# Attention scores in four groups of 32 queries with four heads as rows, in a Griffin-style block on one core

## The chip, the cores and the metric

The kernel runs on one core of a Trainium2 chip. The metric is the device time of one execution in microseconds (us); of the kernel before there are three timed runs, and one further execution that was profiled.

## The reference, cut to what matters

One layer of a decoder over 2048 tokens of width 1024: an RMS norm, one wide projection, two branches (a gated causal convolution and sliding-window attention), each with its own output projection, a gated merge, an output projection and the residual. The change touches the attention alone:

```python
q = rms_norm(q.reshape(b, s, 16, 64), q_norm_g)          # 16 query heads of 64
k = rms_norm(k.reshape(b, s, 4, 64), k_norm_g)           # 4 key/value heads: 4 query heads share one
# per block of 128 queries: keys of this block and of the block before it
scores = einsum('bnqhgd,bnkhd->bnhgqk', qb, kb) * scale
valid = (diff >= 0) & (diff < 128) & (k_pos >= 0)         # diff = q_pos - k_pos
scores = where(valid, scores, -1e30)
m = maximum(max(scores, axis=-1), sink)                   # sink: one learned number per query head
p = exp(scores - m)
p = p / (sum(p) + exp(sink - m))
out = einsum('bnhgqk,bnkhd->bnqhgd', p, vb)
```

A query sees its own position and the 127 before it, so 128 keys in all.

## The kernel before, in words

All matmuls are in fp32r with both operands split in a high and a low part; a product is the sum of three matmuls (high by high, high by low, low by high). The tokens are worked in two halves `t` of 1024. In each half a list of units (`SEQ0`, `SEQ1`) sets which slice of the wide weights is multiplied next; a unit is seven products of 12 matmuls (L475), written by a two-level block scheme that saves one product in eight. `run` counts a tick per product, and `put(n, f)` hangs every other step on a tick. What is recorded stands in each engine's queue in just this order: the schedule is manual, the queues are in order.

The attention is 32 pairs per half (`j`: key/value head, 0 to 3; `b`: block of 128 queries, 0 to 7), 64 blocks in all. `AT0` and `AT1` give the tick `n` of each block, and the steps of a block are at fixed distances from it: `att_load` at n-5, `att_scores` at n, `att_exp` at n+1, `att_norm` at n+2, `att_flip` at n+2, `att_back` at n+4, `att_turn` at n+9, `att_low` at n+10, `att_values` at n+13, `att_out` at n+14, `att_sum` at n+15.

The queries come out of their units with head dimension on rows; `parts` (in `fin_q`) splits them and writes them to DRAM (`q2d`, DMAs on the GpSimd queue, high part on rows 0 to 63, low part on 64 to 127). `k_out` does so for the keys (`kd`), both parts twice so that they fill 128 rows. `att_load` (SP queue) fetches a block's queries and keys. Before, `q2d` keeps groups of 64 queries, and a row of scores is one of two heads by 64 queries; the other pair of heads (`c`) goes to other columns. `att_scores` then runs, for each half `h` of the block's queries, one matmul for the low parts of the keys, with both pairs of heads on the 128 rows and keys that stand block-diagonally in the tiles `lows` (zeros elsewhere), 2 x 192 columns wide, and two matmuls of 192 columns with the high parts of the keys against both parts of the queries. 192 columns are 64 queries' window: 64 keys more than a query sees. `copy_predicated` puts the scores of the first 64 columns in place of the masked ones of the last 64, so that `exp` and all behind it work on 128 columns per row.

`att_exp` computes the sink's term and the weights (four `exp` with `accum_out`), `att_norm` divides, `att_flip` turns 32x32 blocks on VectorE and writes them to DRAM, `att_back` reads them turned, `att_low` masks with four `affine_select` on GpSimd, `att_values` multiplies with the values, `att_out` copies the result out of PSUM.

The rms of the queries: `rms` collects sums of squares, and `by_query` lays the factors out in the tile `rq`, one per score row. For the first three `j` of the first half (`BY_PE`) the queries are turned by TensorE, and `by_query` has to move factors between partitions; for the others `squares_sum` adds two halves of the head dimension.

Of the kernel before, what the change touches and what calls it, by code (L numbers as in the profile page):

```python
# [10 lines left out]
I32 = mybir.dt.int32  # L11
# [42 lines left out]
TURN_WAIT = 3  # L54

# [46 lines left out]
def block_kernel(  # L102
# [49 lines left out]
    q2d = [[dram.tile([P, 2 * NB, 2, 2, HD], F32, name=f"q2d{t}_{j}") for j in range(NKV)]  # L152
# [32 lines left out]
    mask_f = slot([P, 2, HD], F32, "mask_f")  # L185
    for h in range(2):
        nc.gpsimd.affine_select(
            out=mask_f[:, h, :], in_=ones[:, 0:HD], pattern=[[1, HD]], compare_op=ALU.is_gt,
            fill=0.0, base=h * HD, channel_multiplier=-1)
    mask_i = consts.tile([P, HD], I32, name="mask_i")  # L190
    for h in range(2):
        nc.gpsimd.tensor_copy(mask_i[HALVES[h]], mask_f[HALVES[h], h, :])
    negc = consts.tile([P, HD], F32, name="negc")
# [3 lines left out]
    sink_r = cols[:, C_S:NC].rearrange("p (j h c) -> p j h c", h=2, c=2)  # L197
    nsink_r = consts.tile([P, NKV, 2, 2], F32, name="nsink_r")
# [591 lines left out]
    def squares_sum(a, name):  # L790


        got = small.tile([P, 32], F32, tag="sm", name=f"{name}_g")
        both = small.tile([P, 32], F32, tag="sm", name=f"{name}_b")
        av = a.rearrange("p (m s) -> p s m", s=2)
        for k in range(4):
            nc.scalar.copy(got[QUADS[k]], av[QUADS[k ^ 1], k % 2])
        return both, [
            lambda k=k: nc.vector.tensor_tensor(
                out=both[QUADS[k]], in0=av[QUADS[k], k % 2], in1=got[QUADS[k]], op=ALU.add)  # L800
            for k in range(4)]

    def fin_q(t, j):
# [38 lines left out]
        def parts(i, q, qt):  # L842
# [5 lines left out]
            for e in range(2):  # L848
                for half, src in ((LH, hi), (UH, lo)):
                    nc.gpsimd.dma_start(  # L850
                        q2d[t][j][half, q * 2 * HB : (q + 1) * 2 * HB, i, e, :],
                        src[HALVES[e]].bitcast(F32).rearrange("p (b x) -> p b x", x=HD))
# [9 lines left out]
        def by_query(r):  # L862

            rq = consts.tile([P, 2, HB, 2, 2], F32, tag="rq", bufs=4, name=f"rq{t}_{j}")
            if not by_pe:
                vec.tensor_copy(rq, r.rearrange("p (c q b h) -> p q b h c", c=2, q=2, h=2))
# [3 lines left out]
            for e in range(2):  # L870
                for h in range(2):
                    vec.tensor_copy(rq[HALVES[e], :, :, h, :], rv[HALVES[h], :, :, :, e])
# [71 lines left out]
    lows = [consts.tile([P, 2, 2 * P], F32R, name=f"lows{i}") for i in range(2)]  # L944
    for kz in lows:
        nc.gpsimd.memset(kz.bitcast(F32), 0.0)

    def att_load(t, j, b):
        nm = f"{t}_{j}_{b}"
        gb = t * NB + b  # L950
        kz = lows[(j * NB + b) % 2]
        q2 = slot([P, 2, 2, P], F32R, f"q2_{nm}")
        nc.sync.dma_start(
            q2.bitcast(F32).rearrange("p h c x -> p (h c x)"),
            q2d[t][j][:, 2 * b : 2 * b + 2].rearrange("p h c e x -> p (h c e x)"))
# [15 lines left out]
        return q2, kq, kz  # L971
# [18 lines left out]
    def att_scores(t, j, b, ld):  # L990
        first = t * NB + b == 0
        nm = f"{t}_{j}_{b}"
        q2, kq, kz = ld
        rv = rqs[t, j][:, b // HB, b % HB]
        sp = ps_s.tile([P, 2, 2, 2 * P], F32, tag="s", name=f"s{nm}")
        for h in range(2):
            skip = (2 - h) * HD if first else 0
            keys = slice(h * HD + skip, (h + 3) * HD)
            nc.tensor.matmul(
                sp[:, h, :, skip : 3 * HD], lhsT=kq[:, 1, h * P : (h + 1) * P], rhs=kz[:, :, keys],  # L1000
                start=True, stop=False)
            for c in range(2):
                nc.tensor.matmul(  # L1003
                    sp[:, h, c, skip : 3 * HD], lhsT=q2[:, h, c, :], rhs=kq[:, 0, keys],
                    start=False, stop=c == 1)
        sg = sp.rearrange("p h c k -> p (h c) k")
        m = mask_i.unsqueeze(1).to_broadcast([P, G, HD])
        if first:
            vec.copy_predicated(
                sg[:, :, 2 * HD : 3 * HD], m, negc.unsqueeze(1).to_broadcast([P, G, HD]))  # L1010
            vec.tensor_copy(sg[:, 0:2, HD : 2 * HD], negc.unsqueeze(1).to_broadcast([P, 2, HD]))
# [3 lines left out]
        vec.tensor_reduce(out=st[:, 0], in_=sg[:, :, HD : 3 * HD], axis=AX.X, op=ALU.max)  # L1015
# [717 lines left out]
```

## Time and profile before

| | |
|---|---|
| three timed runs | 1894.27, 1896.89, 1897.73 us; median 1896.89 |
| the profiled execution's own time | 1898.81 us |
| its span, first to last instruction | 1897.1 us |
| busy: TensorE, its weight loads | 99%, 83% |
| busy: VectorE, ScalarE, GpSimd | 81%, 52%, 38% |
| DMA | 434.74 MB, mean 229 GB/s |

In rows of the profile PE is TensorE's matmul, PEld its weight load, DVE VectorE, ACT ScalarE, POOL GpSimd, SPq the SP queue. A row's form `128*128 128x192` says that the matmul uses 128 x 128 of the array and writes 128 rows of 192 columns. Line numbers are those of the kernel before.

### The profile page before, as it was taken

How to read it: one execution, taken by the hardware profiler on the slowest of the kernel's cores; microseconds unless marked ns; L12 is line 12 of the kernel's file. 1: busy time of each engine (PE TensorE's matmuls, PEld its weight loads, DVE VectorE, ACT ScalarE, POOL GpSimd, SP SyncE). 2: the span in 40 equal slices, each digit the busy share in tenths (PEclk: the TensorE clock that was granted, in tenths of full speed). 3: DMA queues.
4: the chain of work that ended last, by engine and by line, in shares of the span. 5: the costliest groups of instructions: out<-in, count | busy, mean ns of one | idle time of the engine just before them, and what ended most of it. 6: DMA issues, size and time to landing. Idle time of an engine off the chain costs nothing.

```text
span 1897.1 us, 27925 instructions
## 1 busy us (share of the span) xinstructions
PE 1884.8 (99%) x8670; PEld 1567.5 (83%) x8670; DVE 1537.5 (81%) x2527; ACT 989.6 (52%) x1993; POOL 720.7 (38%) x1022
## 2 busy tenths in 40 slices
PE   9999999999999999999999999999999999999999
PEld 7888888888888887778887888888888888888887
DVE  7989888789777789887579988888888779886654
ACT  7665554567675354345445645556566446444321
POOL 1472454556765121121055445655666311121000
PEclk9999999999999999999999999999999999999999
DMA  8585466689988878989367657767989869889653
GB/s 305 123 211 178 141 175 190 183 258 283 261 239 231 298 267 293 317 290 301 114 186 183 182 174 198 209 182 214 246 234 266 269 237 344 323 273 279 223 174 110
DMA packets 260548, 434.74 MB, mean 229 GB/s; under 512 B 33264, under 2 KB 124400, under 8 KB 260400
## 3 DMA queue, kind: packets, MB, share of 16 engines
q1 hardware_dynamic: 202848, 314.13, 50.8%
q0 software_dynamic: 57408, 118.80, 24.7%
q8 instruction: 69, 1.13, 0.3%
q14 instruction: 79, 0.65, 0.1%
q10 hardware_dynamic: 144, 0.03, 0.0%
HBM read 278.43 MB, written 154.40 MB: 228 GB/s over the span
## 4 chain that ended last, share of the span: by engine, by line
PE 81%; DVE 5%; issue 5%; DMA 5%; POOL 2%; ACT 1%; SPq 0%; DVEq 0%; POOLq 0%; ACTq 0%
PE Y L475 29%; PE Vcv L475 5%; PE Xcv L475 4%; PE Xb L475 2%; PE Xga L475 2%; PE Vb L475 2%; PE Xz L475 2%; PE Vga L475 2%; PE Vz L475 2%; PE Vo L475 2%; PE Xo L475 2%; PE po L1093 2%; PE Vyb L475 2%; PE Xgb L475 2%; PE Xyb L475 2%
## 5 line engine op out<-in xcount | busy, mean ns | idle before, releaser
L1055 POOL DMA_DIRECT2D x<-fd x256 | 142.8, 595 | 79.8 <-DMA fd<-f 30.8
L1076 POOL TENSOR_SCALAR_AFFINE_SELECT xh<-xh 64x512 fp32r<-64x512 f32 x64 | 67.2, 1051 | 137.4 <-DVE xl L257 103.4
L1028 ACT ACTIVATE p<-s,st,rq 128x128 f32<-128x128 f32 x256 | 112.9, 451 | 5.1 <-DMA fd<-f 3.3
L1048 POOL DMA_DIRECT2D fd<-f x64 | 38.6, 604 | 170.6 <-DVE f L257 161.3
L475 PE MATMUL Xcv<-oph,wcv_ah 128*128 128x512 f32 x256 | 79.5, 392 | 0.0
L1109 POOL DMA_DIRECT2D od<-o x64 | 68.9, 1084 | 20.1 <-DMA od<-o 18.1
L1299 POOL DMA_DIRECT2D md<-thyb x32 | 27.4, 873 | 100.6 <-DVE thyb L257 69.8
L1076 POOL TENSOR_SCALAR_AFFINE_SELECT xl<-xl 64x512 fp32r<-64x512 f32 x64 | 63.3, 989 | 4.4
L1076 POOL TENSOR_SCALAR_AFFINE_SELECT yp<-xl 64x512 fp32r<-64x512 f32 x64 | 58.0, 906 | 3.1
L1076 POOL TENSOR_SCALAR_AFFINE_SELECT yp<-yp 64x512 fp32r<-64x512 f32 x64 | 54.7, 855 | 4.2
L475 PEld LDWEIGHTS Xcv<-oph,wcv_ah 128*128 128x128 f32 x256 | 47.3, 188 | 9.4
L257 DVE SCALAR_TENSOR_TENSOR y<-u,cols,y 128x512 f32<-128x512 f32 x64 | 51.8, 810 | 3.7 <-ACT y L1138 2.5
L850 POOL DMA_DIRECT2D q2d<-q_h x64 | 44.2, 691 | 27.9 <-ACT q_h L845 22.8
L257 DVE TENSOR_TENSOR opa<-ina,opa 128x512 fp32r<-128x512 f32 x56 | 36.1, 686 | 20.5 <-ACT opa L292 20.5
L257 DVE TENSOR_TENSOR p<-p,st 128x512 f32<-128x512 f32 x64 | 50.1, 784 | 2.6
L357 ACT CAST wcv_sh<-wcv_raw 128x1024 fp32r<-128x1024 f32 x16 | 16.9, 1054 | 67.1 <-DVE wcv_raw L257 67.1
L1028 ACT ACTIVATION_READ_ACCUMULATOR p<-s,st,rq 128x1 f32 x256 | 51.1, 200 | 0.0
L850 POOL DMA_DIRECT2D q2d<-q_l x64 | 44.1, 689 | 16.8 <-DVE q_l L257 10.2
L475 PE MATMUL Xcv<-oph,wcv_al 128*128 128x512 f32 x128 | 49.8, 389 | 0.0
L1003 PEld LDWEIGHTS s<-kq,q 128*128 128x128 f32 x256 | 45.9, 189 | 2.2
L257 DVE STREAM_TRANSPOSE f<-p 128x512 f32<-128x512 f32 x64 | 45.4, 710 | 2.7 <-DVE p L257 0.2
L257 DVE TENSOR_TENSOR opc<-inc,opc 128x512 fp32r<-128x512 f32 x56 | 36.2, 686 | 13.7 <-ACT opc L292 13.6
(768 smaller groups left out, 6606.1 us busy)
## 6 DMA issues: line engine op xcount, KB each, us to landing
wcv_raw<-in_w_in SPq DMA_DIRECT2D x32, 512.0 KB, 4.2
q<-q2d SPq DMA_DIRECT2D x64, 256.0 KB, 4.7
v<-vd SPq DMA_DIRECT2D x128, 128.0 KB, 4.5
fd<-f POOLq DMA_DIRECT2D x64, 256.0 KB, 3.9
x<-fd POOLq DMA_DIRECT2D x256, 64.0 KB, 3.4
gd<-th SPq DMA_DIRECT2D x64, 256.0 KB, 3.5
wq_raw<-in_w_in SPq DMA_DIRECT2D x16, 512.0 KB, 5.2
q2d<-q_h POOLq DMA_DIRECT2D x64, 128.0 KB, 4.6
```

The costliest lines, as they stand in the source:

```text
L257: r = f(*args, **kw)
L357: return (lambda: nc.scalar.copy(hi, src), lambda: vec.tensor_tensor(out=lo, in0=src, in1=hi.bitcast(F32), op=ALU.subtract))
L475: nc.tensor.matmul(ps, lhsT=w[:, j, :], rhs=b[:, m, :], start=start and j == 0 and i == 0, stop=j == KP - 1 and i == 2, skip_group_check=n ...
L850: nc.gpsimd.dma_start(q2d[t][j][half, q * 2 * HB : (q + 1) * 2 * HB, i, e, :], src[HALVES[e]].bitcast(F32).rearrange("p (b x) -> p b x", x ...
L1003: nc.tensor.matmul(sp[:, h, c, skip : 3 * HD], lhsT=q2[:, h, c, :], rhs=kq[:, 0, keys], start=False, stop=c == 1)
L1028: nc.scalar.activation(out=p[:, i, :], in_=sg[:, i, HD : 3 * HD], func=AF.Exp, bias=st[:, 1, i : i + 1], scale=rv[:, i // 2, i % 2 : i % 2 ...
L1048: nc.gpsimd.dma_start(fd, f)
L1055: nc.gpsimd.dma_start(x[QUADS[k]], src[k])
L1076: nc.gpsimd.affine_select(out=d4, in_=s4, pattern=[[0, 2], [-32 * sg, 2], [0, G], [-sg, 32]], compare_op=ALU.is_gt if prev else ALU.is_ge, ...
L1093: nc.tensor.matmul(po[:, cs], lhsT=v2[:, kind, :], rhs=xx[:, :, h * HD : (h + 1) * HD], start=h == 0 and n == 0, stop=n == 2, skip_group_c ...
L1109: put(tick[0] + ADD_WAIT, lambda: nc.gpsimd.dma_start(to, o[UH].rearrange("p c e q -> p (c e) q"), accum_op=ALU.add))
L1299: nc.gpsimd.dma_start(md[t][k, :, hs(q)], m, accum_op=ALU.add)
```

## The change

Scores are computed for four groups `s` of 32 queries. A row is now one of the four heads by 32 queries, a group's window is 160 keys, and there are two matmuls a group: 128 rows (high and low parts of the queries by the keys' high parts, 160 columns) and 64 rows (queries' high part by the keys' low part, 160 columns). The block-diagonal tiles `lows` and the extra copy of the queries' high parts (`kq`'s second half) go; the low parts of the keys are written and read once, on 64 rows. `q2d` holds runs of 32 elements in place of 64. The masks follow: `copy_predicated` works on 4 x 32 columns. The addition that made the sink's argument goes, since `exp` takes the sink as its bias (a row has one head now). `att_flip` needs three transposes for its four heads' order, `by_query` 16 small copies on ScalarE and GpSimd in place of 4 on VectorE, `squares_sum` 8 copies on ScalarE and one addition in place of 4 and 4. The host's layout of the sinks follows.

```diff
+SLOTS = (0, 1, 2, 3)
-    q2d = [[dram.tile([P, 2 * NB, 2, 2, HD], F32, name=f"q2d{t}_{j}") for j in range(NKV)]
+    q2d = [[dram.tile([P, 4 * NB, 2, 2, 32], F32, name=f"q2d{t}_{j}") for j in range(NKV)]
...
         for e in range(2):
-            for l, src in enumerate((hi, lo)):
-                nc.gpsimd.dma_start(
-                    kd[t][2 * i + e, :, l, hs(q)].rearrange("(o d) t -> d o t", d=HD),
-                    src[HALVES[e]].bitcast(F32).unsqueeze(1).to_broadcast([HD, 2, H]))
+            nc.gpsimd.dma_start(
+                kd[t][2 * i + e, :, 0, hs(q)].rearrange("(o d) t -> d o t", d=HD),
+                hi[HALVES[e]].bitcast(F32).unsqueeze(1).to_broadcast([HD, 2, H]))
+            nc.gpsimd.dma_start(kd[t][2 * i + e, LH, 1, hs(q)], lo[HALVES[e]].bitcast(F32))
...
         for k in range(4):
-            nc.scalar.copy(got[QUADS[k]], av[QUADS[k ^ 1], k % 2])
+            i, e = divmod(k, 2)
+            for o, dst in enumerate((got, both)):
+                nc.scalar.copy(dst[QUADS[k]], a[QUADS[2 * e + o], i * 32 : (i + 1) * 32])
         return both, [
-            lambda k=k: nc.vector.tensor_tensor(
-                out=both[QUADS[k]], in0=av[QUADS[k], k % 2], in1=got[QUADS[k]], op=ALU.add)
-            for k in range(4)]
+            lambda: nc.vector.tensor_tensor(out=both, in0=both, in1=got, op=ALU.add)]
...
-                        q2d[t][j][half, q * 2 * HB : (q + 1) * 2 * HB, i, e, :],
-                        src[HALVES[e]].bitcast(F32).rearrange("p (b x) -> p b x", x=HD))
+                        q2d[t][j][half, q * 4 * HB : (q + 1) * 4 * HB, i, e, :],
+                        src[HALVES[e]].bitcast(F32).rearrange("p (b x) -> p b x", x=32))
...
-            for e in range(2):
-                for h in range(2):
-                    vec.tensor_copy(rq[HALVES[e], :, :, h, :], rv[HALVES[h], :, :, :, e])
+            for k in range(4):
+                for n, s in enumerate(SLOTS):
+                    copy = nc.gpsimd.tensor_copy if s % 2 else nc.scalar.copy
+                    copy(rq[QUADS[k], :, :, n], rv[QUADS[s], :, :, k // 2, k % 2])
...
-        for c in range(2):
-            nc.sync.dma_start(
-                kq[HALVES[c], 1].bitcast(F32).rearrange("p (h x) -> p h x", h=2),
-                q2d[t][j][LH, 2 * b : 2 * b + 2, c].rearrange("p h e x -> p h (e x)"))
...
             nc.sync.dma_start(kq[:, 0, here].bitcast(F32), kd[kt][j, :, 0, there])
-            for c in range(2):
-                nc.sync.dma_start(kz[HALVES[c], c, here].bitcast(F32), kd[kt][j, HALVES[c], 1, there])
+            nc.sync.dma_start(kq[LH, 1, here].bitcast(F32), kd[kt][j, LH, 1, there])
...
-        for h in range(2):
-            skip = (2 - h) * HD if first else 0
-            keys = slice(h * HD + skip, (h + 3) * HD)
-            nc.tensor.matmul(
-                sp[:, h, :, skip : 3 * HD], lhsT=kq[:, 1, h * P : (h + 1) * P], rhs=kz[:, :, keys],
-                start=True, stop=False)
-            for c in range(2):
-                nc.tensor.matmul(
-                    sp[:, h, c, skip : 3 * HD], lhsT=q2[:, h, c, :], rhs=kq[:, 0, keys],
-                    start=False, stop=c == 1)
+        for n, s in enumerate(SLOTS):
+            skip = P - 32 * s if first else 0
+            keys = slice(32 * s + skip, 32 * s + 5 * 32)
+            to = sg[:, n, skip : 5 * 32]
+            nc.tensor.matmul(
+                to, lhsT=q2[:, s], rhs=kq[:, 0, keys],
+                start=n % 2 == 0, stop=False, skip_group_check=n % 2 == 1)
+            nc.tensor.matmul(
+                to, lhsT=q2[LH, s], rhs=kq[LH, 1, keys],
+                start=False, stop=True, skip_group_check=n % 2 == 1)
...
-            vec.copy_predicated(sg[:, :, 2 * HD : 3 * HD], m, sg[:, :, 0:HD])
+            vec.copy_predicated(sg[:, :, 4 * 32 : 5 * 32], m, sg[:, :, 0:32])
...
-        add(st[:, 2], sink_r[:, j].rearrange("p h c -> p (h c)"), st[:, 1])
...
-        nc.scalar.activation(out=st[:, 3], in_=st[:, 2], func=AF.Exp)
+        nc.scalar.activation(out=st[:, 3], in_=st[:, 1], func=AF.Exp, bias=sink_r[:, j, 0:1])
...
-        vec.transpose(out=f, in_=p.rearrange("p g (b r) -> p b g r", r=32))
+        to = f.rearrange("p (b h s q) -> p b h s q", b=4, h=2, s=2)
+        src = p.rearrange("p (h s) (b r) -> p b h s r", s=2, r=32)
+        vec.transpose(out=to[:, 0:3, :, 0], in_=src[:, 1:4, :, 0])
+        vec.transpose(out=to[:, 3, :, 0], in_=src[:, 0, :, 0])
+        vec.transpose(out=to[:, :, :, 1], in_=src[:, :, :, 1])
...
-            d4 = dst.rearrange("p (e s) (g q) -> p e s g q", s=2, q=32)
-            s4 = src.rearrange("p (e s) (g q) -> p e s g q", s=2, q=32)
+            d4 = dst.rearrange("p g (h s q) -> p (g h) s q", s=2, q=32)
+            s4 = src.rearrange("p g (h s q) -> p (g h) s q", s=2, q=32)
             nc.gpsimd.affine_select(
-                out=d4, in_=s4, pattern=[[0, 2], [-32 * sg, 2], [0, G], [-sg, 32]],
+                out=d4, in_=s4, pattern=[[0, 2 * G], [-32 * sg, 2], [-sg, 32]],
```

How the instructions move is shown at two places. The first is TensorE's queue at the scores of block `j` = 0, `b` = 2 of the first half, between two products of a unit (`s` is the score tile, `q` and `kq` are what `att_load` brought, `Xcv` and `Y` are banks of the unit's products). Before:

```order
L475 MATMUL Xcv_2_1963<-oph_2_3_533,wcv_2_al 128x512
L999 MATMUL s_0_2_2060<-lows_151,kq_0_2_1927 128x2x192
L1003 MATMUL s_0_2_2060<-kq_0_2_1927,q_0_0_2_1925 128x192 x2
L999 MATMUL s_0_2_2060<-lows_151,kq_0_2_1927 128x2x192
L1003 MATMUL s_0_2_2060<-kq_0_2_1927,q_0_0_2_1925 128x192 x2
L475 MATMUL Y<-oph_7_0_910,wcv_2_th 128x512 x2
```

The same place after (L990 has 128 rows of operands, L993 has 64):

```order
L476 MATMUL Xcv_2_1999<-oph_2_3_533,wcv_2_al 128x512
L990 MATMUL s_0_2_2093<-kq_0_2_1964,q_0_0_2_1962 128x160
L993 MATMUL s_0_2_2093<-kq_0_2_1964,q_0_0_2_1962 128x160
L990 MATMUL s_0_2_2093<-kq_0_2_1964,q_0_0_2_1962 128x160
L993 MATMUL s_0_2_2093<-kq_0_2_1964,q_0_0_2_1962 128x160
L990 MATMUL s_0_2_2093<-kq_0_2_1964,q_0_0_2_1962 128x160
L993 MATMUL s_0_2_2093<-kq_0_2_1964,q_0_0_2_1962 128x160
L990 MATMUL s_0_2_2093<-kq_0_2_1964,q_0_0_2_1962 128x160
L993 MATMUL s_0_2_2093<-kq_0_2_1964,q_0_0_2_1962 128x160
L476 MATMUL Y<-oph_7_0_910,wcv_2_th 128x512 x2
```

Six matmuls with 1536 columns in all became eight with 1280, of two forms that alternate; the products on both sides stand where they stood.

The second is ScalarE's queue in the first half, where the factors of `j` = 0 are ready (`q_0_r` is VectorE's result, `rq` the tile by query). Before:

```order
L845 ACTIVATE q_1_1_0_h<-q_1_1_0_t,gqk 128x512
L274 ACTIVATE q_0_t<-q_0_ms 128x32
L777 ACTIVATE ptq_1_0_0_1246<-ptq_1_0_0_1246 128x512
L292 CAST k_1_1_h<-pbk_1_1_1252 128x512
L577 COPY q_2_0_1_t<-Vq_2_1138 128x512
```

The same place after:

```order
L845 ACTIVATE q_1_1_0_h<-q_1_1_0_t,gqk 128x512
L275 ACTIVATE q_0_t<-q_0_ms 128x32
L873 COPY rq_0_1241<-q_0_r 32x8 x8
L778 ACTIVATE ptq_1_0_0_1258<-ptq_1_0_0_1258 128x512
L293 CAST k_1_1_h<-pbk_1_1_1264 128x512
L578 COPY q_2_0_1_t<-Vq_2_1138 128x512
```

Eight copies that wait for VectorE's result now stand ahead of the evacuations of PSUM (`ptq`, `pbk`, `Vq`); eight more stand in GpSimd's queue, and VectorE's four are gone.

More of the change, by code (lines that the diff above doesn't have):

```diff
@@ L183, in block_kernel @@
     nc.gpsimd.memset(ones, 1.0)
-    mask_f = slot([P, 2, HD], F32, "mask_f")
-    for h in range(2):
+    mask_f = slot([P, 4, 32], F32, "mask_f")
+    for k in range(4):
         nc.gpsimd.affine_select(
-            out=mask_f[:, h, :], in_=ones[:, 0:HD], pattern=[[1, HD]], compare_op=ALU.is_gt,
-            fill=0.0, base=h * HD, channel_multiplier=-1)
-    mask_i = consts.tile([P, HD], I32, name="mask_i")
-    for h in range(2):
-        nc.gpsimd.tensor_copy(mask_i[HALVES[h]], mask_f[HALVES[h], h, :])
-    negc = consts.tile([P, HD], F32, name="negc")
+            out=mask_f[:, k, :], in_=ones[:, 0:32], pattern=[[1, 32]], compare_op=ALU.is_gt,
+            fill=0.0, base=k * 32, channel_multiplier=-1)
+    mask_i = consts.tile([P, 32], I32, name="mask_i")
+    for k in range(4):
+        nc.gpsimd.tensor_copy(mask_i[QUADS[k]], mask_f[QUADS[k], k, :])
+    negc = consts.tile([P, 3 * 32], F32, name="negc")
     nc.gpsimd.memset(negc, NEG)
-    sink_r = cols[:, C_S:NC].rearrange("p (j h c) -> p j h c", h=2, c=2)
-    nsink_r = consts.tile([P, NKV, 2, 2], F32, name="nsink_r")
+    sink_r = cols[:, C_S:NC].rearrange("p (j s) -> p j s", s=4)
+    nsink_r = consts.tile([P, NKV, 4], F32, name="nsink_r")
     gqk = consts.tile([P, 1], F32, name="gqk")
```

50 lines of the change are left out of this document (22 added, 28 removed).

## The prediction

> **What bounds the kernel now.** The page comes first, for who is busy; then TensorE's waits, then the long runs of its chain, then its queue around one block of scores.
>
> ```profile
> PE 1884.8 (99%) x8670; PEld 1567.5 (83%) x8670; DVE 1537.5 (81%) x2527; ACT 989.6 (52%) x1993; POOL 720.7 (38%) x1022
> PEclk9999999999999999999999999999999999999999
> PE Y L1467 <- DVE zero L176: 1.5, 1, 1.5
> ...
> PE Vya L475 <- ACT zas L1259: 0.2, 1, 0.2
> PE Y L475 <- DVE wya_tl L257: 0.2, 1, 0.2
> 883.18 5.44 PE Xga L475 x24
> 888.62 5.44 PE Vga L475 x24
> ```
>
> TensorE is busy for 99% of the span, with at least nine tenths of its clock granted in every slice. Its waits are ten rows, of which the first is the longest and these the last; none of the ten names a tile of the attention. Undisturbed, 24 matmuls of 512 columns take 5.44 us, 0.227 us each, and the chain is made of such runs. So nothing but TensorE's own instructions sets the end: what they grow by is paid in full, and a saving elsewhere brings next to nothing. What the attention costs here is the spacing of its matmuls, which their durations don't tell, since they overlap. The queue around a late block shows it, matmuls first, weight loads second:
>
> ```profile
> 1452.07 0.34 PE L999 MATMUL s<-lows,kq 128*128 128x384 f32 x1
> 1452.25 0.36 PE L1003 MATMUL s<-kq,q 128*128 128x192 f32 x2
> 1452.45 0.36 PE L999 MATMUL s<-lows,kq 128*128 128x384 f32 x1
> 1452.65 0.36 PE L1003 MATMUL s<-kq,q 128*128 128x192 f32 x2
> 1452.85 0.64 PE L475 MATMUL Xz<-oph,wz_ah 128*128 128x512 f32 x2
> 1452.07 0.37 PEld L1003 LDWEIGHTS s<-kq,q 128*128 128x128 f32 x2
> 1452.36 0.19 PEld L999 LDWEIGHTS s<-lows,kq 128*128 128x128 f32 x1
> 1452.47 0.37 PEld L1003 LDWEIGHTS s<-kq,q 128*128 128x128 f32 x2
> 1452.76 0.30 PEld L475 LDWEIGHTS Xz<-oph,wz_ah 128*128 128x128 f32 x2
> ```
>
> Each load goes out when the matmul before starts to stream. A pair of loads of 0.19 us that spans 0.37 us is 0.18 us apart: its second waits for the 384 columns to stream (384 x 0.227/512 = 0.17 us). The load after that comes 0.11 us later (1452.25 to 1452.36), the next again 0.11 (1452.36 to 1452.47). But 192 columns stream in 192 x 0.227/512 = 0.085 us: there it is no longer the columns that set the pace, it is the next matmul's weights, one load per 0.11 us. That floor decides this change.
>
> **The change part by part.** *TensorE, on the path.* Now a block takes twice 0.18 + 0.11 + 0.11 us = 0.80 us by its loads (the matmuls say 1452.85 - 1452.07 = 0.78). Afterwards there are eight matmuls of 160 columns, which stream in 160 x 0.227/512 = 0.071 us, all of them below the floor. If the floor holds for all, a block takes 8 x 0.11 = 0.88 us: 0.08 us more, though it streams 256 columns fewer. Over 64 blocks that is **+5.1 us**. No row here has a load of 64 rows, or a matmul on 64 rows: every form reads `128*128`. The 64-row load is bounded from below by nothing but the stream it hides behind (0.071 us; then a block takes 4 x 0.11 + 4 x 0.071 = 0.72 us, -4.9 us in all) and from above by what the full one takes. I take the full one, as the nearest row.
>
> The Trainium skill, "TensorE: Matmul & The Clock Gate", section "LDWEIGHTS (loading the stationary operand)", says that a weight load costs its columns divided by 1.2 GHz and not its rows, which for 128 columns is an estimated 0.107 us for 64 rows as for 128; by it the sum would be the same to within 2 us. The 0.11 us above agree for 128 rows; for 64 no run here shows it yet.
>
> *VectorE, off the path.* A block loses the sink's addition and half the elements of `copy_predicated`, and gets two more transposes of the same 512 elements.
>
> ```profile
> L257 DVE STREAM_TRANSPOSE f<-p 128x512 f32<-128x512 f32 x64 | 45.4, 710 | 2.7 <-DVE p L257 0.2
> L257 DVE COPY_PREDICATED s<-mask_i,s 128x256 f32<-128x256 int32 x60 | 25.4, 422 | 6.2 <-PE s L1003 5.7
> L257 DVE TENSOR_TENSOR st<-cols,st 128x4 f32<-128x4 f32 x64 | 17.0, 266 | 2.1
> L257 DVE SCALAR_TENSOR_TENSOR st<-st,nsink_r 128x4 f32<-128x4 f32 x64 | 13.2, 206 | 2.0
> ```
>
> Saved: 266 ns, and of 422 between 0 and 211. Added: twice an instruction's fixed part, between 0 and the 206 ns of a four-element row. Per block that is -477 to +146 ns, so -31 to +9 us over 64 blocks on an engine with 19% to spare; the strided pattern of the transposes could cost more, which no row shows. I take it as nothing on the path. If that cover were gone, the +9 us would be the price.
>
> *ScalarE, nearly off the path.* Twenty-four copies for three `rq` and four more for each of five `squares_sum`, at the 0.218 us of the row below, are 9.6 us on an engine that is half idle. What matters is that the first eight of each `rq` wait for VectorE, with evacuations queued behind:
>
> ```profile
> L797 ACT COPY q_g<-qss x20: 214/218/229, 158.3 to 1082.8; 32x32 f32<-32x32 f32 x20
> 110.83 0.23 ACT L274 ACTIVATE q_t<-q_ms 128x32 f32<-128x32 f32 x1 [1.51 <-DVE q_ms L270]
> 114.00 0.59 ACT L577 COPY q_t<-Vq 128x512 f32<-128x512 f32 x1 [1.94 <-issue]
> 111.93 0.19 DVE L288 SCALAR_TENSOR_TENSOR q_r<-q_t,q_r 128x32 f32<-128x32 f32 x1
> ```
>
> VectorE has the factors at 112.12; eight copies end at 113.9, and the square and the cast that ScalarE did meanwhile (0.6 us each) end at 115.1, so `Vq` is copied out some 1.1 us later than at 114.00. TensorE writes that bank again only after other products of 2.7 us each (12 x 0.227), which hide it. Uncovered it would be 3 x 1.1 = 3 us, once per `rq`.
>
> *GpSimd, SP and the DMAs, off the path.* The same number of `q2d` DMAs now have twice as many runs, half as long:
>
> ```profile
> L850 POOL DMA_DIRECT2D q2d<-q_h x64 | 44.2, 691 | 27.9 <-ACT q_h L845 22.8
> L1048 POOL DMA_DIRECT2D fd<-f x64 | 38.6, 604 | 170.6 <-DVE f L257 161.3
> DMA  8585466689988878989367657767989869889653
> q1 hardware_dynamic: 202848, 314.13, 50.8%
> q0 software_dynamic: 57408, 118.80, 24.7%
> q2d<-q_h POOLq DMA_DIRECT2D x64, 128.0 KB, 4.6
> kq<-q2d SPq DMA_DIRECT2D x128, 64.0 KB, 4.2
> lows<-kd SPq DMA_DIRECT2D x112, 64.0 KB, 3.5
> ```
>
> Their issue goes from 691 ns to at most 691 + (691 - 604) = 778 ns: 128 x 0.09 = 11 us of an engine that idles for 62%. SP issues 128 loads of `q2d` and half of those of `lows` less, and what they moved (8.4 + 3.7 MB of q1, whose 314 MB take 50.8% of the span, 3.07 us a MB) gives 37 us of all the queues' time back. The writes cost, at q0's average of 24.7% of 1897 us for 118.8 MB, 16.8 MB x 3.9 = 66 us; doubled runs cost between nothing and as much again. Half of these 66 us would fall in each half's query units (slices 1 to 3, at 5, 8 and 5 tenths, and about 21 to 23), where room remains. The nearest evidence that lateness there is harmless is that none of TensorE's ten waits is for a DMA. I take nothing.
>
> *The sum.* The profiled execution took 1898.81 us around a span of 1897.1; with +5.1 it is 1903.9. The median of the three timed runs lies 1.9 us lower, at 1896.89, so I forecast **1902.0 us**, 0.27% over before. What a measurement of this kernel can tell from no change is about 0.2%, 3.8 us.
>
> **The rivals.** *A, the array drains between the two forms.* In each block 128-row and 64-row matmuls alternate, eight changes of form. If a matmul of the other form must wait until the one before has left the array, each change costs up to a matmul's whole duration:
>
> ```profile
> L1003 PE MATMUL s<-kq,q x256: 221/263/277, 158.4 to 1452.7; 128*128 128x192 f32 x120, 128*128 128x64 f32 x4, 128*128 128x128 f32 x4
> L1003 PEld LDWEIGHTS s<-kq,q x256: 187/188/192, 158.4 to 1452.6; 128*128 128x128 f32 x128
> ```
>
> At 0.25 us for 160 columns (between 0.221 and 0.263) a block takes 8 x 0.25 = 2.0 us, +1.2, times 64 = +77: 1974 us. If the load can't be hidden either, 8 x (0.25 + 0.19) = 3.5 us a block, +174: 2071 us. A short drain, within the 0.04 us by which the load already outlasts the stream, would vanish in the forecast. For it: nothing here shows the two forms side by side, so nothing speaks against. Against it: the durations' ends are modelled, and back to back they cost nothing today. The Trainium skill, "TensorEngine Tiling (Array Packing)", section "Key Properties", says that changing the tiling mode, not only the tile, drains TensorE; no run here shows it, and it gives no figure. Chance 0.33, a third of it beyond 1974 us.
>
> *B, faster: the 64-row loads are cheap and the columns count.* One mechanism, in TensorE's queue: if a load of half the rows takes half the time, 0.055 us, it hides behind the 0.071 us of streaming, and the block takes the 0.72 us above: -4.9 us, 1892 us. If the short matmuls escape the floor altogether, 8 x 0.071 = 0.57 us, -0.23 x 64 = -15: 1882 us. It decides from a 64-row load under 0.09 us: then 4 x 0.11 + 4 x 0.09 = 0.80 us, as now. Against it stands that the floor of 0.11 us followed the load and not the columns in each row above. Chance 0.09.
>
> *C, the query units become the bound.* If the doubled runs double the cost of `q2d`'s writes, each half's query units have 33 us more DMA time; where 0.65 of 76 us are taken (50 us), that makes 83, and 7 us overflow into waits for weights in each half: with the +5.1, 1916 us. With late evacuations it is 1919. For it: slice 2 at 8 tenths. Against it: 37 us of other traffic go. Chance 0.08.
>
> **How the numbers follow.** The forecast has 0.50. Its own spread, from loads of 0.105 to 0.115 us a piece, is +2.6 to +7.7 us, so 1899.5 to 1904.6 us; about a quarter of it lies within 0.2%. Slower by over 0.2%: 0.37 of the forecast, all but 0.02 of A's 0.33, 0.07 of C: 0.75. Within 0.2%: 0.13 + 0.02 + 0.01, with 0.01 of B: 0.17. Faster: 0.08. The range runs from 1892, where B's milder case lies, to 1974, A without exposed loads; left out are A's worse third (0.11) and half of B (0.04).
>
> **What would show it.** In the profile after, in TensorE's queue: eight score matmuls in 0.88 us, with loads 0.11 us apart for both forms, means that the floor holds. Loads of the 64-row form closer than 0.09 us mean B. Starts of alternate forms over 0.12 us apart mean A, and the spacing is its price. TensorE waiting for a weight tile between 60 and 145 us or 975 and 1070 us means C, or for `Vq`'s bank, the copies. The forecast is wrong if a block of scores isn't within 0.05 us of 0.88 us, or if waits of TensorE beyond today's ten rows come to more than 3 us.

## The result, and the profile after

| | before | after |
|---|---|---|
| median of the runs, us | 1896.35 (4 runs) | 1989.18 (4 runs, 1986.45 to 1991.4) |
| ratio, 95% interval | 1 | 1.0487 [1.0475, 1.0499] |
| profiled execution, us (span) | 1898.81 (1897.1) | 1988.47 (1986.7) |

The changed kernel is 4.9% slower. The forecast of 1902.0 us had the sign; the time lies 15 us above the range's upper end of 1974 us.

The page of the kernel after, its line of engines and its two rows for the score matmuls (busy, mean ns of one, idle before):

```profile
PE 1971.8 (99%) x8798; PEld 1609.4 (81%) x8798; DVE 1515.7 (76%) x2572; ACT 1004.1 (51%) x2037; POOL 737.0 (37%) x1048
L993 PE MATMUL s<-kq,q 64*128 64x160 f32 (+3 forms) x256 | 85.9, 336 | 0.0
L990 PE MATMUL s<-kq,q 128*128 128x160 f32 (+3 forms) x256 | 80.1, 313 | 0.0
```

TensorE is as busy as before, at 99%, and nearly the whole difference shows up as busy time: 1971.8 - 1884.8 = 87 us. VectorE's busy time fell by 22 us, and that bought nothing. The block that the prediction showed, in TensorE's timeline of the kernel after (start, duration), matmuls first, then loads:

```profile
1539.99 0.24 PE L990 MATMUL s<-kq,q 128*128 128x160 f32 x1
1540.15 0.34 PE L993 MATMUL s<-kq,q 64*128 64x160 f32 x1
1540.42 0.34 PE L990 MATMUL s<-kq,q 128*128 128x160 f32 x1
1540.69 0.34 PE L993 MATMUL s<-kq,q 64*128 64x160 f32 x1
...
1541.77 0.34 PE L993 MATMUL s<-kq,q 64*128 64x160 f32 x1
1542.04 0.73 PE L476 MATMUL Xz<-oph,wz_ah 128*128 128x512 f32 x2
1542.61 0.39 PE L476 MATMUL Xz<-oph,wz_al 128*128 128x512 f32 x1
1540.15 0.18 PEld L993 LDWEIGHTS s<-kq,q 64*128 64x128 f32 x1
1540.42 0.19 PEld L990 LDWEIGHTS s<-kq,q 128*128 128x128 f32 x1
1540.69 0.18 PEld L993 LDWEIGHTS s<-kq,q 64*128 64x128 f32 x1
```

Two things are to be seen. The starts of alternate forms are 0.27 us apart (1540.15, 1540.42, 1540.69), not 0.11. And each load starts together with its own matmul: it did not go out while the matmul before it streamed, as the loads did in the kernel before. The block takes 1542.04 - 1539.99 = 2.05 us, where it took 0.78. The effect reaches one matmul further: the first two matmuls of `Xz`, which again have 128 rows, together take 0.73 us where they took 0.64. Added up over all 64 blocks in the two traces, from the first score matmul to the second matmul behind the block, the time went from 65.2 to 151.6 us: 86.4 of the 89.6 us by which the span grew.

The first block of each key/value head in the first half has fewer columns. There the intervals between the forms are 0.21 us at 32 columns, 0.23 at 64, 0.24 at 96 and 0.26 at 128 (the same trace): some 0.2 us that do not depend on the columns, and the streaming on top, by the 0.227 us for 512 columns.

TensorE's waits after have two rows of the attention that before's had not:

```profile
PE po L1087 <- POOL yp L1070: 1.2, 1, 1.2
PE po L1087 <- POOL xl L1070: 0.7, 1, 0.7
```

They are 1.9 us here. In the experiments they turned out to be the tip of a second cost. TensorE also waits twice for ScalarE to empty the bank `Y` (1.0 us), which it did not before.

### The profile page after: what moved, and what is told of

It is laid out like the page before. It is cut to its first block, busy times and chain, and to the rows that moved or that the text cites. A ratio compares the mean times of both kernels' runs of the same rounds, so it can differ in the third digit from the quotient of the medians.

```text
span 1986.7 us, 27990 instructions
## 1 busy us (share of the span) xinstructions
PE 1971.8 (99%) x8798; PEld 1609.4 (81%) x8798; DVE 1515.7 (76%) x2572; ACT 1004.1 (51%) x2037; POOL 737.0 (37%) x1048
## 4 chain that ended last, share of the span: by engine, by line
PE 84%; DVE 5%; DMA 4%; issue 3%; POOL 2%; ACT 1%; SPq 0%; POOLq 0%; DVEq 0%; ACTq 0%
PE Y L476 29%; PE Vcv L476 4%; PE Xcv L476 4%; PE s L993 3%; PE s L990 3%; PE po L1087 2%; PE Xgb L476 2%; PE Vgb L476 2%; PE Xb L476 2%; PE Xga L476 2%; PE Vb L476 2%; PE Xz L476 2%; PE Vga L476 2%; PE Vz L476 2%; PE Xza L476 2%
## 5 line engine op out<-in xcount | busy, mean ns | idle before, releaser
L993 PE MATMUL s<-kq,q 64*128 64x160 f32 (+3 forms) x256 | 85.9, 336 | 0.0
L990 PE MATMUL s<-kq,q 128*128 128x160 f32 (+3 forms) x256 | 80.1, 313 | 0.0
L850 POOL DMA_DIRECT2D q2d<-q_l x64 | 52.8, 824 | 46.4 <-issue 32.1
L993 PEld LDWEIGHTS s<-kq,q 64*128 64x128 f32 x256 | 46.8, 183 | 27.6 <-issue 9.3
L850 POOL DMA_DIRECT2D q2d<-q_h x64 | 52.9, 827 | 41.5 <-issue 19.1
L990 PEld LDWEIGHTS s<-kq,q 128*128 128x128 f32 x256 | 47.8, 187 | 18.0
L1070 POOL TENSOR_SCALAR_AFFINE_SELECT xl<-xl 64x512 fp32r<-64x512 f32 x64 | 57.6, 901 | 4.4
L258 DVE STREAM_TRANSPOSE f<-p 128x192 f32<-128x192 f32 (+2 forms) x192 | 53.5, 328 | 2.8 <-DVE p L258 0.2
L258 DVE SCALAR_TENSOR_TENSOR y<-u,cols,y 128x512 f32<-128x512 f32 x64 | 51.2, 801 | 3.9 <-ACT y L1132 2.7
L258 DVE COPY_PREDICATED s<-mask_i,s 128x128 f32<-128x128 int32 x60 | 17.6, 293 | 45.5 <-PE s L993 45.4
```

The source lines that it names most:

```text
L258: r = f(*args, **kw)
L850: nc.gpsimd.dma_start(q2d[t][j][half, q * 4 * HB : (q + 1) * 4 * HB, i, e, :], src[HALVES[e]].bitcast(F32).rearrange("p (b x) -> p b x", x ...
L990: nc.tensor.matmul(to, lhsT=q2[:, s], rhs=kq[:, 0, keys], start=n % 2 == 0, stop=False, skip_group_check=n % 2 == 1)
L993: nc.tensor.matmul(to, lhsT=q2[LH, s], rhs=kq[LH, 1, keys], start=False, stop=True, skip_group_check=n % 2 == 1)
L1070: nc.gpsimd.affine_select(out=d4, in_=s4, pattern=[[0, 2 * G], [-32 * sg, 2], [-sg, 32]], compare_op=ALU.is_gt if prev else ALU.is_ge, fil ...
```

## The experiments

Two explanations compete for the 87 us. **Change of form**: what costs is the step from a matmul on 128 rows to one on 64 and back, so the time follows the number of steps. **The 64-row matmul itself**: it, or its load, is slow wherever it stands, so the time follows the number of such matmuls, whatever their order. A third possibility is that neither matters, and the eight loads or the rest of the change cost it.

### One form only

The low parts' product is made on 128 rows: the keys' low parts lie in a tile whose upper half is zero.

```diff
-            nc.sync.dma_start(kq[LH, 1, here].bitcast(F32), kd[kt][j, LH, 1, there])
+            nc.sync.dma_start(kz[LH, here].bitcast(F32), kd[kt][j, LH, 1, there])
...
-                to, lhsT=q2[LH, s], rhs=kq[LH, 1, keys],
+                to, lhsT=q2[:, s], rhs=kz[:, keys],
```

> The low-part matmuls of the changed kernel run on 128 rows instead of 64 (the keys' low parts lie in a tile whose rows 64 to 127 are zero); eight matmuls of 160 columns a block, all of one form, the rest of the change as it is. Theory F (each change between the 64-row and the 128-row form costs, nothing else does): no change of form is left, so a block takes the floor of 8 x 0.11 = 0.88 us, +5 us over the kernel before: about 1902 us. Rival P (eight short matmuls that accumulate in turn on the same PSUM columns are slow in any form): stays near 1985 us. Rival R (the other parts of the change cost a share): between the two, with the part over 1902 as their price.

Measured: 1918.74 us, 1.0099 [1.0078, 1.012] of before's 1897.59. Eight matmuls of 160 columns in the same order, with eight loads, cost 70 us less than in the changed kernel. Its timeline of a late block:

```profile
1473.05 0.24 PE L995 MATMUL s<-kq,q 128*128 128x160 f32 x1
1473.13 0.28 PE L998 MATMUL s<-lows,q 128*128 128x160 f32 x1
1473.24 0.27 PE L995 MATMUL s<-kq,q 128*128 128x160 f32 x1
...
1473.80 0.28 PE L998 MATMUL s<-lows,q 128*128 128x160 f32 x1
1473.91 0.67 PE L476 MATMUL Xz<-oph,wz_ah 128*128 128x512 f32 x2
```

The floor of 0.11 us is there, and the block takes 0.86 us against the 0.88 that I had forecast. By the sum over 64 blocks that is 72.1 - 65.2 = 6.9 us. The other 14 of these 21 us, which I had not expected here either, are the second cost, below.

### Fewer changes, the same matmuls

The eight matmuls of the changed kernel in another order: four on 128 rows, then four on 64 (two changes a block); or two and two (four changes).

```diff
+        for n, l, last in [(n, 0, False) for n in range(4)] + [(n, 1, True) for n in range(4)]:
+            work[n][l](last)
```

```diff
+        for n, l, last in ((0, 0, False), (1, 0, False), (0, 1, True), (1, 1, True), (2, 0, False), (3, 0, False), (2, 1, True), (3, 1, True)):
+            work[n][l](last)
```

> The changed kernel with the same eight matmuls a block in another order: four of 128 rows, then four of 64 rows. Theory F: the changed kernel has 8 changes of form a block for +92 us, of which 5 are the floor's, so a change costs 87 / 512 = 0.17 us; here 2 changes a block remain: 5 + 64 x 2 x 0.17 = +27 us, about 1923 us. Rival S (a 64-row matmul or its weight load is slow by itself, whatever its neighbours are): the same 256 of them, unchanged near 1985 us.

> The changed kernel with its eight matmuls a block in the order two of 128 rows, two of 64, two of 128, two of 64. Theory F: 4 changes of form a block, 5 + 64 x 4 x 0.17 = +49 us, about 1945 us, halfway between the grouped order and the changed kernel on a straight line of 22 us per two changes. Rival S: near 1985 us.

| changes of form a block | kernel | us | the 64 blocks in the trace, us |
|---|---|---|---|
| 0 | one form | 1918.74 | 72.1 |
| 2 | four and four | 1933.16 | 92.0 |
| 4 | two and two | 1951.5 | 111.8 |
| 8 | the changed kernel | 1989.18 | 151.6 |

The last three have the same 64-row matmuls, so the 64-row matmul as such isn't it. The blocks (summed as above) grow by 19.9, 19.8 and 39.8 us: 9.9 us a change over 64 blocks, 0.155 us each, on a straight line. By the times it is 70.4 us from 0 to 8 changes, 0.14 us each, and the steps of 14.4, 18.3 and 37.7 us are less even, since the second cost is larger in the first two kernels: outside the blocks the four traces take 1846, 1844, 1834 and 1835 us. Both middle kernels came out above what I expected (1923 and 1945 us). The timeline of "four and four", where rows of one form are drawn together:

```profile
1490.44 0.58 PE L992 MATMUL s<-kq,q 128*128 128x160 f32 x4
1490.94 0.67 PE L995 MATMUL s<-kq,q 64*128 64x160 f32 x4
1491.55 0.73 PE L476 MATMUL Xz<-oph,wz_ah 128*128 128x512 f32 x2
1490.32 0.54 PEld L992 LDWEIGHTS s<-kq,q 128*128 128x128 f32 x4
1490.94 0.52 PEld L995 LDWEIGHTS s<-kq,q 64*128 64x128 f32 x4
```

Four loads on 64 rows of 0.18 us span 0.52: (0.52 - 0.18)/3 = 0.113 us apart, as far as the full ones, (0.54 - 0.19)/3 = 0.117. The first 64-row load stands at the start of its matmul (1490.94 both), the first full one 0.12 us ahead of its own. So it is the step from form to form that takes the load's cover away, and not the 64 rows. The Trainium skill, "TensorE: Matmul & The Clock Gate", section "LDWEIGHTS (loading the stationary operand)", has a load cost its columns and not its rows; these rows agree.

### The price, put into the kernel before

One matmul is added to each block of the kernel before, on 64 rows in the first and on 128 rows in the second, its control. It writes 64 columns that a later matmul overwrites; no part of the computation is left out.

```diff
+        nc.tensor.matmul(
+            sp[:, 0, 0, 2 * HD : 3 * HD], lhsT=kq[LH, 1, 0:P], rhs=kz[LH, 0, 2 * HD : 3 * HD],
+            start=True, stop=True)
```

```diff
+            sp[:, 0, 0, 2 * HD : 3 * HD], lhsT=kq[:, 1, 0:P], rhs=kz[:, 0, 2 * HD : 3 * HD],
```

> The kernel before with one matmul more a block, ahead of its scores: 64 rows, 64 columns, its result overwritten by the scores. Theory F (a change of form costs; from the versions with 0, 2, 4 and 8 changes a block, 70 us for 8, 0.14 us a change): 0.11 us for the matmul and 2 x 0.14 for the two changes, x 64 = +25 us, about 1922 us. Rival N (the price belongs to the new scores' accumulation or order and not to the form): +7 us, like the same matmul on 128 rows, about 1904 us.

> The control: the kernel before with the same extra matmul on 128 rows, one form throughout. One weight load at the floor, 0.11 x 64 = +7 us, about 1904 us, by both theories; near 1897 us if a short matmul hides among the others, so that the floor is no floor.

Measured: 1919.68 us on 64 rows (1.0113 [1.0098, 1.0129]) and 1903.10 on 128 (1.0029 [1.0017, 1.0041]); before took 1897.64. One more matmul costs 5.5 us, 0.085 us a block; the same one on 64 rows costs 16.6 us more. Over 2 x 64 changes that is 0.13 us a change, in a kernel that has nothing else of the change. In the timeline with the 64-row matmul:

```profile
1454.07 0.39 PE L475 MATMUL Xz<-oph,wz_al 128*128 128x512 f32 x1
1454.38 0.29 PE L996 MATMUL s<-lows,kq 64*128 64x64 f32 x1
1454.61 0.44 PE L1002 MATMUL s<-lows,kq 128*128 128x384 f32 x1
1454.89 0.36 PE L1006 MATMUL s<-kq,q 128*128 128x192 f32 x2
1454.38 0.18 PEld L996 LDWEIGHTS s<-lows,kq 64*128 64x128 f32 x1 [0.35 <-issue]
```

From the start of `Xz`'s matmul of 512 columns to that of the 64-row matmul it takes 0.31 us, not 0.23. Its weight load, for which the trace shows nothing to wait for, comes only then, after 0.35 us without a load. And it takes 0.23 us until the next 128-row matmul starts, though only 64 columns stream.

### Where the other 14 us went: GpSimd's queue

In the kernel with one form, TensorE waits longer for the masks that GpSimd makes (first fence), and the first of those masks comes later. The next fences are each kernel's rows on `q2d`'s DMAs (duration min/median/max, first and last start of both halves together; then GpSimd's idle time ahead of such DMAs, in us and times, that no event explains) and on the masks:

```profile
PE po L1092 <- POOL yp L1075: 3.1, 2, 1.9
PE po L1092 <- POOL xl L1075: 2.1, 2, 1.3
PE po L1092 <- POOL xh L1075: 1.7, 2, 1.1
```

The kernel before:

```profile
L850 POOL DMA_DIRECT2D q2d<-q_h x64: 687/687/729, 63.1 to 1069.2; - x64
  issue: 2.9, 6
L1076 POOL TENSOR_SCALAR_AFFINE_SELECT xh<-xh x64: 742/762/1690, 188.9 to 1483.3; 64x512 fp32r<-64x512 f32 x64
```

The kernel with one form:

```profile
L850 POOL DMA_DIRECT2D q2d<-q_h x64: 822/824/862, 63.3 to 1086.7; - x64
  issue: 48.2, 50
L1075 POOL TENSOR_SCALAR_AFFINE_SELECT xh<-xh x64: 739/762/1673, 197.8 to 1504.4; 64x512 fp32r<-64x512 f32 x64
```

An issue takes 0.82 us where it took 0.69; the doubled runs are all that the change did to these DMAs. The 48.2 us of waits don't follow from that. The last `q2d` DMA of the first half starts at 176.7 us instead of 149.5 (from the traces), GpSimd's part of the copies into `rq` stands behind it, and the masks behind those, the first of them 8.9 us late.

The waits for masks, 6.9 us, are only part of the 14. Behind them the clock that TensorE was granted fell to half, for 3.4 and for 6.8 us. A slice of the page is 48 us long, so its row of the clock doesn't show this. The first two rows are these stretches (start:end and length, TensorE's busy time and matmuls, granted clock, DMA share and GB/s); the third is from TensorE's timeline in the second of them, where 12 matmuls of 512 columns take 5.28 us, 0.44 us each:

```profile
203.40:206.80 3.40, 3.40 (x10) 0.50 0.01 2
1094.30:1101.10 6.80, 6.11 (x16) 0.50 0.37 116
1096.01 5.28 PE L476 MATMUL Y<-oph,wcv_d 128*128 128x512 f32 x12
```

Half of the 9.5 us that TensorE worked at half clock is 4.8 us. All of its waits come to 16.2 us, against 8.4 before, so that is 7.8 us more. Together these are 12.6 of the 14.4 us by which the span grew outside the blocks. In the kernel before the clock was halved only in the last 2 us of the span.

Two explanations for GpSimd's waits: the queue ran out of the scratch that the kernel gives its dynamic DMAs, which now hold twice the runs; or GpSimd is just late, with its longer issues and what they wait for.

Half the writes issued by ScalarE, on top of the kernel with one form:

```diff
-                    nc.gpsimd.dma_start(
+                    (nc.scalar if src is hi else nc.gpsimd).dma_start(
```

> The one-form version of the changed kernel (low parts on 128 rows), with the high parts' writes to q2d issued from ScalarE's queue, so that GpSimd issues 64 instead of 128 of them. Theory G (the 15 us over the forecast in that version come from GpSimd's queue, whose longer q2d writes make the first masks of each half late): the first masks come on time, about 1903 to 1906 us. Rival D (the doubled runs cost DMA time, whoever issues them) or V (the three transposes, the copies): stays at about 1919 us.

More scratch, on top of the same:

```diff
-        "TRN2", target_bir_lowering=False, num_devices=1, dynamic_dma_scratch_size=4096)
+        "TRN2", target_bir_lowering=False, num_devices=1, dynamic_dma_scratch_size=6144)
```

> The one-form version with the scratch space of GpSimd's DMA descriptors raised from 4096 to 6144 bytes, nothing else. Theory G1 (part of GpSimd's lateness is waiting for room for descriptors, of which each q2d write now needs twice as many: 48 us in 50 waits that no semaphore explains): most of those waits go and the time falls by 5 to 13 us, to 1906 to 1914 us. Rival G2 (only the longer issue, 0.82 against 0.69 us, and the waits are for data): unchanged, 1919 us.

More scratch took 11.9 us away: 1906.82 us, 1.0043 [1.003, 1.0057]. Its rows:

```profile
L850 POOL DMA_DIRECT2D q2d<-q_h x64: 822/823/843, 63.5 to 1077.0; - x64
  issue: 19.9, 26
L1075 POOL TENSOR_SCALAR_AFFINE_SELECT xh<-xh x64: 739/764/1673, 191.4 to 1490.2; 64x512 fp32r<-64x512 f32 x64
```

The issue time and the number of DMAs are the same, the waits are down to 19.9 us, and the masks come at 191.4. So most of the lateness was for want of room. TensorE's waits add up to 7.3 us, and its clock is not halved before the span ends: 8.9 and 4.8 us less, of the 14.1 us by which this trace is shorter. (The four runs of the one-form kernel lie between 1910.86 us, at a mean clock of 0.999, and 1920.83, at 0.996, so the 11.9 us carry some of that spread.) What is left over before is 1906.82 - 1898.34 = 8.5 us, of which the blocks are 6.9; so the three transposes, the copies and the longer issues cost no more than some 1.6 us here.

Moving half the writes to ScalarE was a failure: 1941.88 us, 1.0232 [1.0218, 1.0246], 23 us worse than leaving them. TensorE's waits in it:

```profile
PE Y L476 <- DVE q_t L258: 12.1, 3, 6.8
PE Y L476 <- ACT Y L499: 4.9, 5, 2.3
PE Vq L476 <- ACT wq_sh L358: 3.0, 2, 2.5
```

It put new waits for VectorE and ScalarE into the query units, so it says nothing of the room. In the traces TensorE's waits grow by 14.4 us over the kernel with one form, and the stretches at half clock from 10.2 to 23.9 us; the span grows by 20.4. How each of the waits came about, I did not follow.

In the changed kernel itself more room is worth little. With 8192 in place of 4096 and nothing else:

```diff
-        "TRN2", target_bir_lowering=False, num_devices=1, dynamic_dma_scratch_size=4096)
+        "TRN2", target_bir_lowering=False, num_devices=1, dynamic_dma_scratch_size=8192)
```

> The changed kernel with 8192 bytes for GpSimd's DMA descriptors in place of 4096, nothing else. In the one-form version more room took off 12 us, but there TensorE waited for masks; in the changed kernel its own slower scores leave GpSimd more time, and the waits for masks are 2 us. Theory G1: 2 to 6 us less, 1983 to 1987 us; 12 us less (1977) if the lateness was paid in full here too.

1984.95 us, 1.0456 [1.0442, 1.0471]: 4.2 us below the 1989.18 of the changed kernel, beside which before was 1.3 us faster. The waits ahead of `q2d`'s DMAs that no event explains go from 51.2 us, 54 times, to 5.9 us, 11 times, and a stretch of 3.4 us at half clock, behind the waits for masks, is gone. So GpSimd waited for room in the changed kernel as long as in the one with one form (48.2 us), but TensorE waited only 1.9 us for the masks, not 6.9. That its slower score blocks give GpSimd the time to catch up is how I read this; no run isolates it.

### Can the change be kept without its price?

Six matmuls a block: the low parts of two groups in one matmul on 128 rows of 2 x 160 columns, against a tile of keys with zeros off the diagonal, as the kernel before has it; the rest as changed.

```diff
+            if s % 2 == 0:
+                pair = max(skip - 32, 0)
+                nc.tensor.matmul(
+                    sg[:, n : n + 2, pair : 5 * 32], lhsT=kq[:, 1, s * 64 : s * 64 + P],
+                    rhs=kz[:, :, 32 * s + pair : 32 * s + 5 * 32], start=True, stop=False)
             nc.tensor.matmul(
-                to, lhsT=q2[LH, s], rhs=kq[LH, 1, keys],
...
+                sg[:, n, skip : 5 * 32], lhsT=q2[:, s], rhs=kq[:, 0, keys],
```

> The changed kernel with the low parts of two groups of 32 queries in one matmul of 128 rows and 2 x 160 columns, keys block-diagonal as in the kernel before: six matmuls a block, 1280 columns, one form. Theory F with the floor of one weight load per 0.11 us: a block takes 2 x (320 x 0.227/512 + 0.11 + 0.11) = 0.72 to 0.74 us against 0.80 us before, -0.06 to -0.08 x 64 = -4 to -5 us: about 1892 us. If the rest of the change (three transposes, doubled runs, copies on ScalarE) cost anything on the path, 1896 us or more.

1907.87 us, 1.0054 [1.0041, 1.0067], 16 us above the 1892 that I expected. Its blocks are shorter than before's, 61.8 us in all against 65.2 by the same sum over the trace, but GpSimd's waits are there too (49.4 us ahead of `q2d`'s DMAs), and 10.2 us at half clock as in the kernel with one form. So I tried to take these away, first with both means at once: half the writes on ScalarE, and the copies into `rq` on VectorE.

```diff
-                    copy = nc.gpsimd.tensor_copy if s % 2 else nc.scalar.copy
-                    copy(rq[QUADS[k], :, :, n], rv[QUADS[s], :, :, k // 2, k % 2])
+                    vec.tensor_copy(rq[QUADS[k], :, :, n], rv[QUADS[s], :, :, k // 2, k % 2])
```

> The six-matmul version (low parts of two groups in one 128-row matmul) with the high parts' writes to q2d from ScalarE's queue and the 16 copies for rq back on VectorE. Theory G with the floor of one load per 0.11 us: 1908 less the 13 us of waits for masks, about 1893 us, 4 us under the kernel before. If the rest of the change still costs something on the path: 1897 us or more.

1934.92 us, 1.0212 [1.0191, 1.0233]: a miss by 42 us; TensorE stalls in the query units as in the kernel above where ScalarE issues, and it spends 17.1 us at half clock. Next with more scratch (5504, paid for by a smaller `lows` and four buffers less in one pool), and the copies still on VectorE:

```diff
-    small = ctx.enter_context(tc.tile_pool(name="small", bufs=12))
+    small = ctx.enter_context(tc.tile_pool(name="small", bufs=8))
...
-    lows = [consts.tile([P, 2, 2 * P], F32R, name=f"lows{i}") for i in range(2)]
+    lows = [consts.tile([P, 2, 7 * 32], F32R, name=f"lows{i}") for i in range(2)]
...
-        "TRN2", target_bir_lowering=False, num_devices=1, dynamic_dma_scratch_size=4096)
+        "TRN2", target_bir_lowering=False, num_devices=1, dynamic_dma_scratch_size=5504)
```

> The six-matmul version with 5504 bytes for GpSimd's DMA descriptors (the low keys' tiles are cut to the 224 columns used and the pool of small tiles from 12 buffers to 8 to make room) and the 16 copies for rq on VectorE. Six matmuls at 0.74 us against 0.80 are -4 us; with most of the 13 us of late masks gone, 1893 to 1898 us, at or under the kernel before. If 5504 bytes are too few, or the smaller pool makes VectorE wait: 1900 us or more.

1905.03 us, 1.0042 [1.0029, 1.0055], above the 1893 to 1898 us that I expected. Two of its waits for VectorE, of which the first is followed by 3.4 us at half clock, looked like the copies':

```profile
PE Y L476 <- DVE vr L258: 2.1, 1, 2.1
...
PE Y L476 <- DVE q_t L258: 1.5, 1, 1.5
```

The last run has the copies back on ScalarE and GpSimd, as the change put them:

```diff
-                    vec.tensor_copy(rq[QUADS[k], :, :, n], rv[QUADS[s], :, :, k // 2, k % 2])
+                    copy = nc.gpsimd.tensor_copy if s % 2 else nc.scalar.copy
+                    copy(rq[QUADS[k], :, :, n], rv[QUADS[s], :, :, k // 2, k % 2])
```

> The six-matmul kernel with the larger room for descriptors and the smaller lows tiles of e9_six_more_room, but the copies into rq on ScalarE and GpSimd as in the changed kernel. Theory (what is left over 1896.4 us is GpSimd's queue and the copies, no longer TensorE's blocks, which take about 0.73 us against 0.80): putting the copies back takes away the waits for VectorE at 100 to 165 us that VectorE's copies brought, some 5 to 8 us, so 1896 to 1900 us, a tie with the kernel before. Rival (the copies' place is not what those waits came from; they come from the query units' DMAs): 1903 to 1908 us, as with the copies on VectorE.

1898.73 us over 11 runs, 1.0014 [1.0005, 1.0023] of before's 1896.8 over 15. That is 6.3 us below the kernel with VectorE's copies, and both of those waits are gone. It is within 0.2% of before, but the interval leaves it slightly slower. Its runs spread from 1895.25 to 1902.18 us, and the trace is of the fastest. There the block takes 1449.23 - 1448.53 = 0.70 us against 0.78:

```profile
1448.53 0.31 PE L1007 MATMUL s<-lows,kq 128*128 128x320 f32 x1
1448.68 0.35 PE L1010 MATMUL s<-kq,q 128*128 128x160 f32 x2
1448.86 0.35 PE L1007 MATMUL s<-lows,kq 128*128 128x320 f32 x1
1449.05 0.35 PE L1010 MATMUL s<-kq,q 128*128 128x160 f32 x2
1449.23 0.67 PE L476 MATMUL Xz<-oph,wz_ah 128*128 128x512 f32 x2
```

No kernel that I ran beats the one before.

## Why the prediction was wrong, by its steps

**What bounds the kernel: right.** 86.4 of the 89.6 us by which the span grew lie in TensorE's own spacing, in the 64 blocks and the matmul behind each.

**"If the floor holds for all": the step that failed.** The 0.11 us a load came from rows that all read `128*128`, and I carried it over to a pair of forms that no row showed side by side. With one form it holds (0.86 us a block measured, 0.88 forecast; 6.9 us in all, 5.1 forecast). Between forms it doesn't: 0.27 us from start to start, so 2.05 us a block. The forecast's sign was right by luck, since its 5 us had another cause than the 93. Rival A named the cost of each change and the reading that would show it, and both came; its chance of 0.33 was too low. (That the array must empty between the forms is its explanation. The traces fit it, but they show only when loads and matmuls start.) What I put against it, that matmuls cost nothing back to back today, was again seen on one form only, so it was no evidence. The Trainium skill, "TensorEngine Tiling (Array Packing)", section "Key Properties", whose drain on a change of tiling mode stands in the prediction, was the only statement on the case itself; the runs agree with it, as far as starts and times can show it, and add the price.

**Rival A's price, and with it the range: a little low.** 0.25 us a matmul gave 2.0 us a block and +77 us. The block came to 2.05 (in the sum over 64 blocks +81.5 us), and the change back to `Xz`, which I had left out, was 4.9 us more. The rest of the 15 us beyond 1974, some 6, lies outside the blocks; more scratch took away 4.2. That 0.25 came so near is partly luck: I took it from the duration of a matmul, whereas the price is some 0.2 us that don't depend on the columns, and the streaming. The worse case, in which the load is exposed, was left outside the range. The trace shows a load that starts only with its own matmul, but as part of the 0.27 us and not on top of a full duration.

**The 64-row load priced as the full one: right** (0.113 us apart), and so rival B is out.

**VectorE taken as nothing on the path: right.** Its busy time fell by 21.8 us, within the -31 to +9, and no time came back.

**ScalarE's copies nearly hidden: right.** The waits after have no row for `Vq`'s bank. The new 1.0 us for `Y`'s bank is from the other copies: before each of the two waits, at 1046.6 and 1066.8 us, ScalarE makes eight for a `squares_sum` where it made four, which is 0.9 us more ahead of the copy that empties the bank.

**GpSimd, "I take nothing": mis-sized.** The issue went to 0.82 us, over the 0.778 that I gave as its most, since I had scaled it from a DMA of another shape. More important, the waits that came with it were in no step, nor were the stretches at half clock: by the runs with more scratch they cost 12 us in the kernel with one form and 4 in the changed one. My evidence, that TensorE waits for no DMA, looked for the wrong waiter: the DMAs delayed the instructions behind them on GpSimd, and TensorE then waited for GpSimd's masks. Rival C had the place, the query units, but looked for it in the DMAs' traffic.

## What to carry to other kernels

A floor read from a trace holds for the shapes in that trace; when a change mixes a second shape in between, price the step from shape to shape by itself, or keep the shape and pad with zeros, which here cost 0.11 us a matmul against 0.27. If both shapes must be there, group them: two changes a block instead of eight saved 56 us. And when a DMA gets more runs, look at what stands behind it on the engine that issues it. When TensorE's waits have grown, read its granted clock in windows of a few us: the page's slices are too long to show a short loss.

## What the runs showed of the hardware that was not expected

- A change between matmuls on 128 and on 64 rows costs 0.13 to 0.14 us by the times and 0.155 by the spacing in the traces, either way, and the load of the new form starts only with its own matmul; at 160 columns alternate matmuls start 0.27 us apart, at 32 columns 0.21.
- Twice the runs in a DMA raised GpSimd's issue from 0.69 to 0.82 us, and its unexplained waits ahead of those DMAs from 2.9 to 48.2 us; with 6144 in place of 4096 of scratch they were 19.9 us, and in the changed kernel 8192 took them from 51.2 to 5.9 us. That the scratch holds the DMAs' descriptors is my reading of it; shown is only that more of it shortens the waits.
- TensorE's granted clock fell to half for 3.4 to 10.2 us at a time, each time just behind or across a wait of TensorE. Of the 14 traces, the eight in which TensorE's waits add up to 9.7 us or more have such stretches, and the six with 8.4 us or less have none before the last 4 us. That the waits bring the lower clock fits all of them, but no run varies the one without the other.
